# A decoder layer on one core: two gates as a block product ahead of the attention, and four output tiles begun with heads 0 to 3 behind it

## The chip, the core and the metric

The kernel runs on one core of a Trainium2 chip. Five engines work side by side, each through its own queue in order: TensorE (PE) multiplies matrices into PSUM, VectorE (DVE) and ScalarE (ACT) work element by element, GpSimd (POOL) and SyncE (SP) issue transfers here. Loading the stationary operand of a matmul is listed apart as PEld. The metric is the device time of one execution in microseconds.

## The reference

One decoder layer over 1024 tokens of width 1024, in float32. What matters here:

```python
h = rms_norm(x, norm_mix_pre)
proj = h @ w_in                    # q, k, v, u_pool, q_mem, gate logits
a = diff_attention(q, k, v, lam)   # 8 heads, two softmax maps each
a = rms_norm(a, subln_g) * (1.0 - lam_init)
y_attn = a @ w_attn_branch
y_pool = multiscale_pool(...) @ w_pool_branch
y_mem = memory_cross_attention(...) @ w_mem_branch
gates = sigmoid(gate_logits)       # 3 x 1024 columns
mix = gates[0] * y_attn + gates[1] * y_pool + gates[2] * y_mem
x = x + rms_norm(mix @ w_out, norm_mix_post)
# then the channel mixer: w_up, causal conv3, gelu gate, w_down
```

The change concerns `gates[0]`, the gate logits of the attention branch (8 tiles of 128 columns), and the product with `w_attn_branch` (8 output tiles).

## The kernel before

**Products.** Every operand of a product is split into a high and a low part (`split`, L86: a rounding copy on ScalarE, a difference on VectorE), and a product is three matmuls (`mm3`, L102): high by high, high by low, low by high. Tensors have channels on the partitions and tokens along the free axis; the 1024 tokens are two halves of 512, one PSUM bank each. A plain product of one 128-column tile of `w_in` with `h` is 2 halves x 8 depth tiles x 3 = 48 matmuls of 128x512.

**Block products.** `seven` (L198) computes a pair of such tiles in Strassen-Winograd form: depth and columns are cut in two, seven products (`product`, L175, 4 depth tiles x 3 = 12 matmuls each) take the place of eight. That is 84 matmuls for a pair in place of 96. Its weight sums (`weight_sums`, L184) are four VectorE additions; the sums of `h` were made once before (`hops`). `channels` (L1014) loads the weights of a pair and calls `seven`.

**Ahead of the attention** come, in this order: the values (block products), `channels` for the keys of heads 0 and 1, for the queries of heads 0 to 7 in four pairs (results split by `split_heads` and stored to `q_d`), and for gates 0 and 1. `marks["ahead"]` makes the weight sums of the call that follows the keys wait, on VectorE's queue, for the end of the keys' own. The weights of gate 2 are then split (`ready`, L1046).

**The attention** (L1349 on) goes over 8 heads, and in each over 4 blocks of two query tiles of 128. For a tile: `products` (L1164) gives the two score maps; `scores` (L1185) takes score plus bias and its minimum on VectorE (L1203) and the exponential on ScalarE (L1212); `combine` (L1224) joins the two maps on VectorE (L1232); one block later `turn_weights` (L1237) transposes them on TensorE and splits them, and `weigh_values` (L1255) multiplies with the values. A score map fills two banks and there are two such pairs of banks, so the products of a tile wait until the minimum of the tile before has read its map. These steps are the list `stages`; between them `weave` (L259) puts a list of `fillers`, work without a part in that chain: the keys of the next head (`head_keys`, L1105, heads 1 to 6 make those of heads 2 to 7: 48 matmuls in four steps), loads of the next values, and gates. `GATES` (L1347) says which gate fills which head: gates 2 and 3 in head 0, gate 4 in head 7. `gate` (L1135) is a generator of 8 steps of 6 matmuls, each step behind the latest scores; the first steps of gate 2 run ahead of the first scores. A scheduler orders the instructions by program order and readiness; `tc.issue_after` adds an order on one engine's queue.

**Behind the attention** gates 5, 6 and 7 are computed (L1460). Then the eight heads are loaded, scaled by their norms and split (L1470 to L1475, into `ath` and `atl`). Norms of heads 4 to 7 need the last head's squares, a trip through DRAM (`ss_d`, `head_norms`, `r_d`) and a load. `merge_heads(dt, g)` (L1446) multiplies output tile `dt` with heads 0 to 3 (g = 0) or 4 to 7 (g = 1), 24 matmuls each; tiles 0 and 1 get their first half before heads 4 to 7 are loaded. `merge(dt)` (L1493) applies the sigmoid gate and adds the other branches (`mixp_d`). Then follow the loads of `w_out` (`load_wo`, L1486) and the output projection.

## Time and profile before

| what | value |
|---|---|
| median of 3 runs | 1725.25 us (1724.72 to 1725.97) |
| the profiled execution | 1723.22 us |
| its span, first to last instruction | 1721.4 us |
| granted TensorE clock, mean | 1.000 |
| first scores of head 0 | at 601.88 us |
| first merge matmul | at 903.75 us |
| first matmul of the output projection | at 990.84 us |

How to read the profile: a line of the order in time has the start in us, the duration, the engine, the line of the kernel, the operation, what it writes and reads, the size, and in brackets how long the engine had idled before it and what ended that. A line of the groups has the count, the busy time in us and the mean in ns, and the idle time before the group. A line of the stretches has begin and end, length, and the busy time of each engine with its number of instructions, then the granted clock, the share of the transfer engines and GB/s. Durations of matmuls overlap, so the distance between starts is what a matmul takes.

### The profile page before, as it was taken

To read this page: it belongs to the slowest core of one execution; us is meant where nothing else is said; L and a number is where in the kernel's file an instruction comes from. 1 tells how busy PE (TensorE), PEld (TensorE's weight loads), DVE (VectorE), ACT (ScalarE), POOL (GpSimd) and SP (SyncE) were. 2 spreads that over 40 slices of the span, in tenths; PEclk is the share of its full clock that TensorE was granted. 3 is DMA by queue.
4 is the path that set the end of the run, shared out by engine and by line. 5 is a ranking of instruction groups with operands and counts; after the bars stand their busy time and mean duration, and the time that the engine had idled before them with its cause. 6 is when DMAs were issued, how large, how long until landed. Compare 5 with 4: busy or idle time off the path is not lost.

```text
span 1721.4 us, 22406 instructions
## 1 busy us (share of the span) xinstructions
PE 1710.9 (99%) x8106; PEld 1421.0 (83%) x8106; DVE 1241.8 (72%) x2059; ACT 890.0 (52%) x1585; POOL 45.0 (3%) x103
## 2 busy tenths in 40 slices
PE   9999999999999999999999999999999999999998
PEld 6888888888888888888888888888888888888886
DVE  7676876666665578988866555848888888878466
ACT  5434544444544467777744344645555555543453
POOL 0000000000000011111110000000000000000000
PEclk9999999999999999999999999999999999999999
DMA  8675544444874676666466670563433332583344
GB/s 276 242 253 219 163 149 156 160 141 155 257 231 153 209 228 179 179 183 170 117 215 214 204 212 38 180 217 95 126 121 93 122 101 83 199 301 102 107 150 137
DMA packets 232867, 294.41 MB, mean 171 GB/s; under 512 B 15929, under 2 KB 161590, under 8 KB 230070
## 3 DMA queue, kind: packets, MB, share of 16 engines
q1 hardware_dynamic: 229222, 285.61, 52.0%
q0 software_dynamic: 3520, 7.38, 1.2%
q8 instruction: 64, 1.05, 0.2%
q14 instruction: 45, 0.37, 0.1%
q10 hardware_dynamic: 16, 0.00, 0.0%
HBM read 201.10 MB, written 85.56 MB: 167 GB/s over the span
## 4 chain that ended last, share of the span: by engine, by line
PE 97%; DVE 2%; DMA 1%; issue 1%; ACT 0%; DVEq 0%
PE pa L103 8%; PE pa L105 8%; PE pa L104 8%; PE pb L104 5%; PE pb L103 5%; PE pb L105 5%; PE pss L1178 4%; PE poa L1267 3%; PE pd L103 2%; PE pd L104 2%; PE pd L105 2%; PE pta L1248 2%; PE pe L103 2%; PE pe L105 2%; PE pe L104 2%; PE pout L103 2%
## 5 line engine op out<-in xcount | busy, mean ns | idle before, releaser
L89 ACT ACTIVATE wpage<-s 128x512 fp32r<-128x512 f32 x136 | 85.3, 627 | 103.2 <-PE pb L105 33.6
L1655 DVE SCALAR_TENSOR_TENSOR cvt<-gv,cols,cvt 128x1023 f32<-128x1023 f32 x88 | 112.5, 1278 | 14.8 <-ACT cvt L1651 14.8
L90 DVE TENSOR_TENSOR wpage<-s,wpage 128x512 fp32r<-128x512 f32 x136 | 92.8, 688 | 39.7 <-ACT wpage L89 39.7
L1203 DVE CUSTOM_DVE_ANT_0 z<-pss,hbias 128x256 f32<-128x256 f32 (+7 forms) x128 | 94.6, 752 | 22.4 <-PE pss L1178 19.9
L1212 ACT ACTIVATE z<-z,mx 128x256 f32<-128x256 f32 (+7 forms) x128 | 98.8, 773 | 22.4 <-DVE mx L1203 22.0
L103 PE MATMUL pa<-T,wpage 128*128 128x512 f32 x264 | 102.9, 390 | 0.3 <-DVE gv L252 0.3
L105 PE MATMUL pa<-T,wpage 128*128 128x512 f32 x264 | 102.7, 389 | 0.0
L104 PE MATMUL pa<-T,wpage 128*128 128x512 f32 x264 | 102.7, 389 | 0.0
L89 ACT ACTIVATE page<-blk 128x1024 fp32r<-128x1024 f32 (+1 forms) x42 | 41.4, 989 | 86.3 <-PE pe L104 50.6
L1178 PE MATMUL pss<-ks,q 128*128 128x512 f32 (+5 forms) x384 | 83.9, 347 | 1.1 <-DVE mx L1203 1.0
L90 DVE TENSOR_TENSOR page<-blk,page 128x1024 fp32r<-128x1024 f32 (+1 forms) x42 | 47.5, 1131 | 39.5 <-ACT page L89 39.5
L1178 PEld LDWEIGHTS pss<-ks,q 128*128 128x128 f32 x384 | 63.5, 188 | 9.0 <-DVE mx L1203 3.2
L103 PE MATMUL pd<-page 128*128 128x512 f32 x176 | 68.7, 390 | 0.0
L104 PE MATMUL pd<-page 128*128 128x512 f32 x176 | 68.5, 389 | 0.0
L105 PE MATMUL pd<-page 128*128 128x512 f32 x176 | 68.3, 389 | 0.0
L103 PE MATMUL pa<-hT,wpage 128*128 128x512 f32 x168 | 65.5, 390 | 0.0
L105 PE MATMUL pa<-hT,wpage 128*128 128x512 f32 x168 | 65.4, 389 | 0.0
L104 PE MATMUL pa<-hT,wpage 128*128 128x512 f32 x168 | 65.4, 389 | 0.0
L1267 PEld LDWEIGHTS poa<-aT,v 128*128 128x128 f32 x480 | 61.2, 190 | 3.7 <-ACT srow L1294 1.8
L1267 PE MATMUL poa<-aT,v 128*128 128x256 f32 (+1 forms) x480 | 63.3, 281 | 0.0
L103 PEld LDWEIGHTS pa<-T,wpage 128*128 128x128 f32 x264 | 49.6, 188 | 11.2 <-DVE gv L252 0.7
L104 PEld LDWEIGHTS pa<-T,wpage 128*128 128x128 f32 x264 | 49.6, 188 | 10.2
(429 smaller groups left out, 4970.5 us busy)
## 6 DMA issues: line engine op xcount, KB each, us to landing
q<-q_d SPq DMA_DIRECT2D x64, 256.0 KB, 4.6
wd<-in_w_down_dram SPq DMA_DIRECT2D x22, 512.0 KB, 5.7
tw_d<-wd SPq DMA_DIRECT2D x11, 1024.0 KB, 4.0
rawv<-in_w_up_dram SPq DMA_DIRECT2D x22, 512.0 KB, 5.7
rawu<-in_w_up_dram SPq DMA_DIRECT2D x22, 512.0 KB, 4.0
ff_d<-cvt SPq DMA_DIRECT2D x22, 512.0 KB, 4.7
blk<-ff_d SPq DMA_DIRECT2D x20, 512.0 KB, 6.2
br<-tw_d SPq DMA_DIRECT2D x20, 512.0 KB, 4.2
```

Of the source, the lines that this page charges most:

```text
L89: copy = nc.scalar.activation(out=hi, in_=src, func=AF.Copy)
L90: nc.vector.tensor_tensor(out=lo, in0=src, in1=hi.bitcast(F32), op=ALU.subtract)
L103: nc.tensor.matmul(o, ah, bh, start=first, stop=False, skip_group_check=onto)
L104: nc.tensor.matmul(o, ah, bl, start=False, stop=False, skip_group_check=onto)
L105: return nc.tensor.matmul(o, al, bh, start=False, stop=last, skip_group_check=onto)
L1178: last["scores"] = nc.tensor.matmul(pss[:, i * H:i * H + m], q[:, j, c, ts], keys, start=(j == 0), stop=(j == 1))
L1203: last["min"] = nc.vector.tensor_tensor_reduce(out=halves(z[:, 0:n]), in0=pss.rearrange("p (a m) -> p a m", a=2)[:, 0:parts, 0:m], in1=hal ...
L1212: last["exp"] = nc.scalar.activation(out=z[:, 0:n], in_=z[:, 0:n], func=AF.Exp, scale=-1.0, bias=mx[:, c:c + 1], accum_out=sm if c else su ...
L1248: nc.tensor.transpose(pt[:, j * P:(j + 1) * P], zs[u][:, k * P:(k + 1) * P], ident)
L1267: nc.tensor.matmul(po[:, qs], (vh, vl)[i][:, k, :], w[j][:, ws], start=(n == 0), stop=(n == len(terms) - 1))
L1655: nc.vector.scalar_tensor_tensor(out=cv[:, sh:], in0=u[:, 0:S - sh], scalar=w, in1=cv[:, sh:], op0=ALU.mult, op1=ALU.add)
```

## The change

Gates 2 and 3 are computed by `channels` as one pair, between the keys of heads 0 and 1 and the queries, and stored to `gate_d`. The plain gates that fill the attention move up: gate 4 fills head 0, alone, and gate 5 head 7; gates 6 and 7 remain behind the attention. In head 0 one gate step and one load of values change places. The key weights of head 2 are loaded early (`fetch_keys`). In head 7 one step of gate 5 goes ahead of the last score products. Behind the attention, weights of the output tiles are loaded and split by halves (`merge_weights`); four tiles, in place of two, are multiplied with heads 0 to 3 before heads 4 to 7 are loaded, head by head; then tiles 0 and 1 take heads 4 and 5 and after that 6 and 7. Tiles 2, 3, 6 and 7 accumulate in the double banks. The last loads of `w_out` are queued behind the last load of `mixp_d`.

```diff
         marks["ahead"] = marks["c22"]
+        g = channels(C_G + 2 * P)
+        nc.sync.dma_start(out=gate_d[2:4].rearrange("e p s -> p e s"), in_=g)
         for h in range(0, NH, 2):
             split_heads(channels(h * P), q_d[h:h + 2], -0.125)
...
-        ready = {2: wsplit(chunk(w_in, C_G + 2 * P), [P, KT, P])}
-        with tc.issue_after(ready[2][2].ins):
+        ready = {4: wsplit(chunk(w_in, C_G + 4 * P), [P, KT, P])}
+        with tc.issue_after(ready[4][2].ins):
             late[0]()
...
+    fetched = {}
+
+    def fetch_keys(h):
+        w2 = [wst.tile([P, KT, P], F32R, tag=t, name=t) for t in ("wh", "wl")]
+        with tc.issue_after(last["keys"].ins):
+            for e, w in enumerate(w2):
+                nc.sync.dma_start(out=w.bitcast(F32), in_=wk_d[h, :, e])
+        return w2
...
-        wh, wl = [wst.tile([P, KT, P], F32R, tag=t, name=t) for t in ("wh", "wl")]
-        with tc.issue_after(last["keys"].ins):
-            for e, w in enumerate((wh, wl)):
-                nc.sync.dma_start(out=w.bitcast(F32), in_=wk_d[h, :, e])
+        wh, wl = fetched.pop(h) if h in fetched else fetch_keys(h)
...
-            for ins in calm if dt == 5 else ():
+            for ins in calm if dt == 6 else ():
...
-    first = gate(2)
+    first = gate(4)
...
-        ready[3] = wsplit(chunk(w_in, C_G + 3 * P), [P, KT, P])
     load_keys(1)
     last["keys"] = last["load"]
-    GATES = ((2, 3), (), (), (), (), (), (), (4,))
+    fetched[2] = fetch_keys(2)
+    gates = {}
+    GATES = ((4,), (), (), (), (), (), (), (5,))
...
-                stages.append(lambda h=h, b=b: scores(h, b, 0, ready[3][2] if (h, b) == (0, 2) else None))
+                stages.append(lambda h=h, b=b: scores(h, b, 0, None))
...
-                        products(h, b, 1)
+                        if h == NH - 1:
+                            next(gates[5])
+                            with tc.issue_after(last["gate"].ins):
+                                products(h, b, 1)
+                        else:
+                            products(h, b, 1)
...
-                        ready[4] = wsplit(chunk(w_in, C_G + 4 * P), [P, KT, P])
+                        ready[5] = wsplit(chunk(w_in, C_G + 5 * P), [P, KT, P])
...
-            for step in steps(first if dt == 2 else gate(dt), 5 if dt == 2 else 8):
+            gates[dt] = first if dt == 4 else gate(dt)
+            for step in steps(gates[dt], 5 if dt == 4 else 8):
                 fillers.insert(min(n, len(fillers)), step)
                 n += 2
+        if h == 0:
+            fillers[3:5] = fillers[4], fillers[3]
...
-    def merge_heads(dt, g):
+    def merge_weights(dt, g, own=None):
+        raw = wst.tile([P, HG, P], F32, tag="raw", name="rawm", bufs=2)
+        nc.sync.dma_start(out=raw, in_=w_attn_branch[g * HG * P:(g + 1) * HG * P, dt * P:(dt + 1) * P]
+                          .rearrange("(k p) c -> p k c", p=P))
+        if own:
+            w = own.tile([P, 2, HG, P], F32R, tag="page", name="mpage", bufs=2)
+        else:
+            w = wst.tile([P, 2, HG, P], F32R, tag=("wh", "wl")[pages[0] % 2], name="mpage")
+            pages[0] += 1
+        split(w[:, 0], w[:, 1], raw)
         if g == 0:
-            pys[dt] = wsplit(chunk(w_attn_branch, dt * P), [P, KT, P])[:2] + (bank(name="pya"), pbank(name="pya"))
-        wh, wl, *py = pys[dt]
+            if dt % 4 < 2:
+                pys[dt] = bank(name="pya"), pbank(name="pya")
+            else:
+                py = bank2(name="pya")
+                pys[dt] = py[:, 0:H], py[:, H:2 * H]
+        return w
+
+    def merge_heads(dt, w, ks):
         for i in range(2):
             hs = slice(i * H, (i + 1) * H)
-            for k in range(g * HG, (g + 1) * HG):
-                mm3(py[i], wh[:, k, :], wl[:, k, :], ath[k][:, hs], atl[k][:, hs], k == 0, k == KT - 1)
+            for k in ks:
+                mm3(pys[dt][i], w[:, 0, k % HG, :], w[:, 1, k % HG, :], ath[k][:, hs], atl[k][:, hs],
+                    k == 0, k == NH - 1)
...
-        for dt in range(5, KT):
+        for dt in range(6, KT):
             for step in steps(gate(dt), 8):
                 step()
+        ws = [merge_weights(dt, 0, sub) for dt in range(2)]
         for h in range(NH):
+            if h == 2:
+                ws += [merge_weights(dt, 0) for dt in range(2, 4)]
             if h == HG:
...
-                for dt in range(2):
-                    merge_heads(dt, 0)
+                for k in range(HG):
+                    for dt in range(4):
+                        merge_heads(dt, ws[dt], (k,))
...
-            nc.sync.dma_start(out=mp, in_=mixp_d[dt][:, hs])
+            last["gm"] = nc.sync.dma_start(out=mp, in_=mixp_d[dt][:, hs])
...
-    for dt in range(KT):
-        if dt >= 2:
-            merge_heads(dt, 0)
-        merge_heads(dt, 1)
+    ws = [merge_weights(dt, 1) for dt in range(2)]
+    for ks in ((4, 5), (6, 7)):
+        for dt in range(2):
+            merge_heads(dt, ws[dt], ks)
+            if ks[0] == 6:
+                merge(dt)
+    for dt in range(2, KT):
+        for g in range(0 if dt >= 4 else 1, 2):
+            merge_heads(dt, merge_weights(dt, g), range(g * HG, (g + 1) * HG))
         merge(dt)
...
-        for k in range(4, KT):
-            load_wo(wo, k)
+        with tc.issue_after(last["gm"].ins):
+            for k in range(4, KT):
+                load_wo(wo, k)
```

More of the change, by code (lines that the diff above doesn't have):

```diff
@@ L1493, in merge @@
     def merge(dt):
-        for i, py in enumerate(pys.pop(dt)[2:]):
+        for i, py in enumerate(pys.pop(dt)):
             hs = slice(i * H, (i + 1) * H)
```

## The prediction

> **What bounds the kernel now.** I read the page first: its busy line, its clock row and its chain.
>
> ```profile
> span 1721.4 us, 22406 instructions
> ...
> PE 1710.9 (99%) x8106; PEld 1421.0 (83%) x8106; DVE 1241.8 (72%) x2059; ACT 890.0 (52%) x1585; POOL 45.0 (3%) x103
> ...
> PEclk9999999999999999999999999999999999999999
> ...
> PE 97%; DVE 2%; DMA 1%; issue 1%; ACT 0%; DVEq 0%
> ```
>
> TensorE carries 97% of the chain, at full clock. Busy time overstates it, since pipelined matmuls overlap: one 128x512 matmul shows 0.39 us. So next I read the order in time on TensorE through the six block-product pairs ahead of the attention, from the first product to the first plain gate matmul.
>
> ```profile
> 484.93 0.39 PE L103 MATMUL pa<-hTh,wpage 128*128 128x512 f32 x1
> ...
> 580.12 0.39 PE L103 MATMUL pa<-hTh,wpage 128*128 128x512 f32 x1
> ...
> 599.16 0.39 PE L103 MATMUL pg<-hTh,wh 128*128 128x512 f32 x1
> 599.39 0.39 PE L104 MATMUL pg<-hTl,wh 128*128 128x512 f32 x1
> ```
>
> Six pairs of 84 matmuls take 599.16 - 484.93 = 114.23 us: **0.2267 us a matmul, 19.04 us a pair**, and the last pair alone takes 19.04 too. Plain gate matmuls follow at the same distance. No pair waits for weights, splits or sums, so a matmul taken out of a dense stretch is worth 0.2267 us.
>
> Is the attention dense as well? The stretches of the eight heads, cut at each head's first score matmul (the last at the end of its last gate matmul), columns PE, PEld, DVE, ACT, POOL:
>
> ```profile
> 601.88:637.44 35.56, 35.56 (x195) 30.27 (x193) 25.09 (x65) 23.16 (x55) 4.46 (x8) 1.00 0.83 241
> 637.44:669.69 32.25, 32.25 (x201) 28.08 (x200) 27.03 (x71) 24.37 (x59) 4.25 (x8) 1.00 0.64 176
> 669.69:702.02 32.33, 32.33 (x201) 28.45 (x200) 28.81 (x73) 25.74 (x63) 4.28 (x8) 1.00 0.62 175
> ...
> 766.70:799.26 32.56, 32.48 (x201) 28.09 (x200) 29.85 (x88) 25.29 (x62) 4.28 (x9) 1.00 0.68 191
> 799.26:831.52 32.26, 32.26 (x201) 28.18 (x200) 29.10 (x73) 25.18 (x62) 4.28 (x9) 1.00 0.61 161
> 831.52:863.46 31.94, 30.86 (x186) 26.69 (x185) 26.44 (x69) 23.16 (x58) 4.53 (x9) 1.00 0.30 83
> ```
>
> TensorE is covered throughout, but VectorE is busy 84 to 92% of each head, and every head is held together by filler: 48 plain matmuls (keys of the next head, or a gate) of 10.88 us, in head 0 the 84 that are left of gates 2 and 3 (12 of gate 2's 48 run before the first scores). Where filler runs out, TensorE waits for VectorE. That happens once, in head 7:
>
> ```profile
> 853.87 1.78 PE L1178 MATMUL pss<-ks,q 128*128 128x448 f32 x8
> 856.69 1.18 PE L1178 MATMUL pss<-ks,q 128*128 128x512 f32 x4 [1.03 <-DVE mx L1203]
> 857.71 0.38 PE L1248 MATMUL pta<-ident,z 128*128 128x128 f32 x2
> 857.85 1.18 PE L1178 MATMUL pss<-ks,q 128*128 128x512 f32 x4
> ```
>
> The last token block's products need the banks that the minimum (L1203) of the block before still reads.
>
> **The change part by part.**
>
> *Gates 2 and 3.* Removed: 2 x 48 = 96 plain matmuls. Added: one pair of 84. At 0.2267 us: -21.76 + 19.04 = **-2.72 us**. The pair also brings seven splits, four weight sums, six evictions, two 512 KB weight loads and one 1 MB store on the SP queue; the four neighbouring pairs hold all of that (theirs with four wide splits and two stores more) inside 19.04 us without a wait, so it costs nothing; if the cover failed, it would show as a gap between pairs. What goes on the other side are two weight splits (1.06 us ACT and 1.22 us VectorE each by the wh and wl rows below), four evictions and four stores issued by POOL.
>
> *Head 0 with 36 filler matmuls instead of 84.* Dense, it would shrink by 48 x 0.2267 = 10.88 us to 24.68 us. Its VectorE work is 25.09 us, of which one weight split goes:
>
> ```profile
> L1203 DVE CUSTOM_DVE_ANT_0 z<-pss,hbias 128x128 f32<-128x128 f32 (+7 forms) x16 | 11.6, 751 | 7.8 <-PE pss L1178 7.8
> ...
> L90 DVE TENSOR_TENSOR wl<-raw,wh 128x1024 fp32r<-128x1024 f32 x1 | 1.2, 1222 | 0.0
> L1229 DVE RECIPROCAL mx<-sm 128x1 f32<-128x1 f32 x8 | 1.2, 158 | 3.0 <-ACT z L1212 3.0
> ```
>
> 25.09 - 1.22 = 23.87 us in 24.68 would be 97% busy, more than any head shows. The 7.8 us that VectorE idles for scores are filler time and go with it; the 3.0 us for exponentials are latency and stay unless other work steps in. Bounds for the length: at 92%, the highest share above (29.85 of 32.56), 26.0 us, a loss of 1.4; at 84%, the lowest (27.03 of 32.25), 28.5 us, a loss of 3.8; at no loss 24.7. I take **+1.4 us**: head 0 starts with empty queues and ends, unlike heads 1 to 6, without the previous head's last transposes. A delay of VectorE at its end may run into head 1, as it does from each head into the next already. The row of head 7 speaks for a loss of this size: 1.03 us at one place where no filler stood.
>
> The Trainium skill, "TensorE: Matmul & The Clock Gate", Part 2, says that only weight loads are pulled ahead and matmuls stay in program order. The trace agrees: behind the wait of 1.03 us stood gate matmuls whose weights had long been split, and none stepped forward. By that rule this change takes away what hides the waits, and the sum has the loss; if matmuls could pass a waiting one, the loss would be 0 and the sum that of rival A.
>
> *Head 7.* One gate step (6 matmuls, 1.36 us) is put ahead of the last products, where the wait of 1.03 us is. The total of filler is unchanged; the six are missing a few us later, where gate 6 can follow at once, as gate 5 does now. **-1.0 us** (from -1.0 to 0).
>
> *Key weights of head 2* (two loads of 512 KB) are issued behind the keys of head 1, near 607 us, instead of at 631; gate 3's weight load (512 KB, 600.41 us) goes.
>
> ```profile
> 600.41 0.48 SPq L337 DMA_DIRECT2D raw<-in_w_in_dram  x1
> 602.09 4.71 SPq L1102 DMA_DIRECT2D ks<-k_d  x4
> 606.90 1.01 SPq L1080 DMA_DIRECT2D v<-v_d  x2
> ...
> 630.93 0.59 SPq L1111 DMA_DIRECT2D wh<-wk_d  x1
> 631.56 0.43 SPq L1111 DMA_DIRECT2D wl<-wk_d  x1
> ```
>
> Behind them wait values(1) and the queries of head 1. 512 KB more at the 241 GB/s of head 0's row is 2.2 us on loads that are needed about 20 us later: cost 0, from 0 to 2.2 if head 1 starts early on late queries.
>
> *Behind the attention.* Before: 144 gate and 48 merge matmuls stand ahead of heads 4 to 7; after: 96 and 96. The cover of the latency chain (squares, norms, r_d, rows of heads 4 to 7) stays 192 matmuls. Now:
>
> ```profile
> 889.15 1.23 DVE L90 TENSOR_TENSOR atl<-a,ath 128x1024 fp32r<-128x1024 f32 x1 [0.57 <-ACT ath L89]
> ...
> 915.45 1.23 DVE L90 TENSOR_TENSOR atl<-a,ath 128x1024 fp32r<-128x1024 f32 x1 [1.13 <-ACT ath L89]
> ```
>
> ```profile
> 903.75 0.39 PE L103 MATMUL pya<-ath,wh 128*128 128x512 f32 x1
> ...
> 914.63 0.39 PE L103 MATMUL pya<-ath,wh 128*128 128x512 f32 x1
> ...
> 916.67 0.39 PE L103 MATMUL pya<-ath,wh 128*128 128x512 f32 x1
> ...
> 990.84 0.39 PE L103 MATMUL pout<-woh,mixh 128*128 128x512 f32 x1
> ```
>
> Head 7 is split at 916.68 and first used at 916.67 + 0.23: just in time. With the new order (heads 4 and 5 for two tiles, then 6 and 7) it is wanted 24 matmuls, 5.44 us, after head 4 plus one head, so the chain gains some 4 us of slack. The early end is tighter: the merge starts one gate (10.88 us) and the 1.0 us of head 7 sooner, at 891.9 on the old axis, and the first head is ready at 890.4. The weights of tiles 2 and 3 are loaded between heads 1 and 2 and split on the queues that split the heads. I take 0; bounds 0 and +2 us, the time by which head 0 would have to slip. The 384 merge matmuls stay dense now (990.84 - 903.75 = 87.09 us = 384 x 0.2268). Sixteen half weight splits for eight whole ones add 1.6 us ACT (16 x 0.63 - 8 x 1.06) and 1.3 us VectorE (16 x 0.69 - 8 x 1.22), spread over 87 us of matmuls with VectorE at about two thirds: hidden. The output projection's last weights now wait for the last mixp load, off the path.
>
> ```profile
> L89 ACT ACTIVATE wpage<-s 128x512 fp32r<-128x512 f32 x136 | 85.3, 627 | 103.2 <-PE pb L105 33.6
> L90 DVE TENSOR_TENSOR wpage<-s,wpage 128x512 fp32r<-128x512 f32 x136 | 92.8, 688 | 39.7 <-ACT wpage L89 39.7
> ...
> L90 DVE TENSOR_TENSOR wl<-raw,wh 128x1024 fp32r<-128x1024 f32 x6 | 7.3, 1220 | 0.8 <-ACT wh L89 0.8
> L89 ACT ACTIVATE wh<-raw 128x1024 fp32r<-128x1024 f32 x6 | 6.3, 1055 | 5.1 <-PE pg L104 4.7 <-PE pya L104 0.4
> ```
>
> **Sum**: -2.72 + 1.4 - 1.0 + 0 = **-2.3 us**. The profiled execution took 1723.22 us, 1.8 more than its span; the median of the three runs is 1725.25, 2.0 higher. All terms are differences, so I set them against the median: **1722.9 us**, -0.14%. 0.2%, about what a measurement of this kernel can tell from no change, is 3.45 us.
>
> **The rivals.**
>
> *A. All dense.* The new order of head 0's filler covers every wait: -2.72 - 1.0 = -3.7 us, 1721.5, just beyond 0.2%. For it: before, head 0 loses under half a us in all its gaps; ACT and VectorE drop a split. Against it: 97% of VectorE. It decides from a loss under 0.3 us in head 0.
>
> *B. Head 0 is paced by VectorE, slower than before.* Heads 1 to 6 take 32.3 us with like work on VectorE. If each block's chain (scores, minimum, exponential, combine, transpose, split) sets the pace and head 0 needs 32.3 us as well, it loses 7.6 us: -2.72 - 1.0 + 7.6 = +3.9, **1729.1**. It is slower beyond 0.2% from a head 0 of 31.9 us on. Against it: heads 1 to 6 have 10.88 us of filler where head 0 keeps 8.16, 3 to 6 us more VectorE work, and are dense, so 32.3 is their TensorE time, not a latency.
>
> *C. Late first merge.* The four tiles begin 11.9 us sooner; if the loads of heads 0 and 1 slip behind the two extra weight loads, or tiles 2 and 3 wait for splits queued behind the heads, TensorE loses 2 us there: 1724.9, no measurable change.
>
> **How the numbers follow.** Forecast (head 0 loses 0.3 to 3.8) 0.52, A 0.28, C 0.08, B or another loss of its size 0.12. Forecast and C lie within 0.2%: faster 0.28, same 0.60, slower 0.12. The range leaves out B alone: from A less the 1.25 us between the lowest and the highest run shown (1724.72 and 1725.97), 1720.2, to the forecast with the upper bounds of head 0 and of the first merge, -2.72 + 3.8 - 1.0 + 2 = +2.1, 1727.3. The forecast's own range, with head 0 alone between its bounds, is 1721.8 to 1725.3.
>
> **What would show it.** Twelve matmuls fewer (8094, less what a trace misses). From the first pair's product to the first plain gate matmul 114.2 + 19.04 = 133.3 us: longer means the pair isn't free. Head 0, between first score matmuls, 26.0 us: 24.7 is A, 32 is B. The wait of 1.03 us at head 7's last products gone. From the first merge matmul to the first of the output projection 87.1 us: longer is C. Wrong would be the whole argument if the time moved by more than 0.2% with these four as forecast, or if a wait showed up outside these stretches.

## The result and the profile after

The changed kernel took **1728.03 us** (median of 12 runs, 1725.45 to 1732.11); the kernel before, on the same chip, 1725.14 us (12 runs, 1723.58 to 1725.97). The ratio is 1.0019, with a 95% interval from 1.0010 to 1.0028: slower by 0.19%, where 0.14% faster was forecast, and 0.7 us above the range.

The profiled execution took 1729.82 us, 1.8 more than its span. The head of its page and its chain:

```profile
span 1728.0 us, 22426 instructions
...
PE 1713.0 (99%) x8094; PEld 1420.0 (82%) x8094; DVE 1249.7 (72%) x2079; ACT 893.5 (52%) x1598; POOL 42.9 (2%) x99
...
PE 90%; DMA 4%; DVE 3%; ACT 1%; SPq 1%; issue 1%; DVEq 0%; ACTq 0%
```

The twelve matmuls are gone (8094). But the chain that ended last runs through TensorE for 90% of the span, where before it was 97%; of the rest DMA has 4%, VectorE 3%, and ScalarE and SP's queue 1% each. The stretches of the changed kernel, cut at the same events as in the prediction, show where; the columns are length, busy time of PE, PEld, DVE, ACT and POOL, granted clock, DMA share and GB/s. In order: first pair product to first gate matmul, head 0, head 1, head 7 to the first merge product, first merge product to the first of the output projection, and from there to the first transpose (pt) behind the first output row.

```profile
486.75:620.03 133.28, 133.28 (x589) 110.39 (x588) 74.57 (x106) 54.80 (x88) 2.81 (x3) 1.00 0.54 175
622.75:650.39 27.64, 27.13 (x152) 21.92 (x151) 23.84 (x64) 21.26 (x52) 3.05 (x6) 1.00 0.95 271
650.39:681.99 31.60, 31.45 (x196) 27.29 (x197) 27.24 (x71) 24.77 (x60) 4.58 (x9) 1.00 0.65 181
843.87:903.76 59.89, 59.82 (x341) 51.06 (x340) 41.82 (x102) 34.70 (x82) 8.84 (x17) 1.00 0.39 116
903.76:991.25 87.49, 87.36 (x386) 71.95 (x385) 56.76 (x73) 37.41 (x54) 0.54 (x1) 1.00 0.66 217
991.25:1018.54 27.29, 23.96 (x97) 18.55 (x96) 13.78 (x21) 10.56 (x15) 0.00 (x0) 0.94 1.09 317
```

The last stretch in the kernel before:

```profile
990.84:1012.61 21.77, 21.77 (x97) 17.97 (x96) 13.41 (x21) 9.49 (x14) 0.00 (x0) 1.00 1.07 292
```

The front does nearly what was said: up to the first merge product the changed kernel is ahead by 1.8 us (903.76 - 486.75 = 417.01 against 903.75 - 484.93 = 418.82), where the sum of the prediction, whose terms other than 0 all lie in this stretch, gave 2.3. Then one place takes 5.5 us: **96 matmuls of the first output row need 27.29 us in place of 21.77**. The other differences are small: 0.4 us in the merges, 0.7 us in all that follows, and 1.8 us ahead of the first pair product, where the two kernels are the same and 20 profiles lie between 484.8 and 486.8 us whatever the kernel. The sum is 1.8 - 1.8 + 0.4 + 5.5 + 0.7 = 6.6 us, the difference of the spans. The medians differ by 2.9, since the profiled execution of before lies 1.9 us under its median and the changed one's 1.8 over.

TensorE's order in time at that place, in the changed kernel:

```profile
996.46 0.39 PE L105 MATMUL pout<-woh,mixl 128*128 128x512 f32 x1
998.95 0.50 PE L103 MATMUL pout<-woh,mixh 128*128 128x512 f32 x1 [2.10 <-ACT woh L89]
1000.21 0.50 PE L104 MATMUL pout<-wol,mixh 128*128 128x512 f32 x1 [0.76 <-DVE wol L90]
1000.55 0.54 PE L105 MATMUL pout<-woh,mixl 128*128 128x512 f32 x1
1000.89 0.63 PE L103 MATMUL pout<-woh,mixh 128*128 128x512 f32 x1
1001.32 0.63 PE L104 MATMUL pout<-wol,mixh 128*128 128x512 f32 x1
...
1003.27 0.80 PE L104 MATMUL pout<-wol,mixh 128*128 128x512 f32 x1 [0.47 <-DVE wol L90]
```

24 products (four rows of w_out) run densely from 991.25 on; then TensorE waits for the high words of row 4, its low words, and the low words of row 5 (six products belong to a row, so 1003.27 is the 32nd). Between the waits, products stand 0.43 us apart, not 0.2267. The granted clock in stretches of 4 us (the column behind POOL):

```profile
996.00:1000.00 4.00, 1.35 (x5) 0.56 (x3) 2.00 (x3) 1.88 (x2) 0.00 (x0) 1.00 0.98 352
1000.00:1004.00 4.00, 3.32 (x8) 2.16 (x9) 3.37 (x5) 2.22 (x4) 0.00 (x0) 0.58 1.03 386
1004.00:1008.00 4.00, 4.00 (x19) 3.23 (x18) 1.57 (x2) 1.06 (x1) 0.00 (x0) 0.99 1.18 296
```

So part of the 5.5 us is a lower clock behind the waits: 0.58 for 4 us.

Why are the rows late? ScalarE's order in the changed kernel:

```profile
987.37 1.13 ACT L89 ACTIVATE mixh<-gm 128x512 fp32r<-128x512 f32 x2
993.06 0.63 ACT L1540 ACTIVATE gm<-gm 128x512 f32<-128x512 f32 x1 [4.55 <-issue]
994.38 0.63 ACT L1540 ACTIVATE gm<-gm 128x512 f32<-128x512 f32 x1 [0.69 <-DMA gm<-gate_d]
997.84 1.06 ACT L89 ACTIVATE woh<-rawo 128x1024 fp32r<-128x1024 f32 x1 [2.83 <-DMA rawo<-in_w_out_dram]
```

And the SP queue, the changed kernel first, the kernel before second:

```profile
982.26 0.33 SPq L1527 DMA_DIRECT2D rawo<-in_w_out_dram  x1
989.35 0.32 SPq L1538 DMA_DIRECT2D gm<-gate_d  x1
989.73 0.42 SPq L1539 DMA_DIRECT2D gm<-mixp_d  x1
990.24 0.38 SPq L1538 DMA_DIRECT2D gm<-gate_d  x1
990.67 1.11 SPq L1539 DMA_DIRECT2D gm<-mixp_d  x1
991.83 1.37 SPq L1527 DMA_DIRECT2D rawo<-in_w_out_dram  x3
```

```profile
982.75 0.33 SPq L1499 DMA_DIRECT2D gm<-gate_d  x1
...
985.47 0.32 SPq L1499 DMA_DIRECT2D gm<-gate_d  x1
985.83 0.43 SPq L1500 DMA_DIRECT2D gm<-mixp_d  x1
986.32 0.42 SPq L1488 DMA_DIRECT2D rawo<-in_w_out_dram  x1
```

The new order holds rows 4 to 7 until the last mixp load is out, 990.67. That alone would not be late: the loads of the last tile themselves go out 1.9 and 1.0 us ahead of the first output product (991.25), before it was 8.1 and 5.4 us. Two things can make them late. A load needs one of two gm buffers, which VectorE gives back at the end of a merge (SP's queue waits 6.7 us for that ahead of 989.35). And tiles 6 and 7 sit in one two-bank tile each, whose halves VectorE multiplies together. VectorE's multiplications of tile 6, L1541, changed, and L1502, before:

```profile
984.21 1.28 DVE L1541 TENSOR_TENSOR gm<-pya,gm 128x512 f32<-128x512 f32 x2
```

```profile
978.55 0.68 DVE L1502 TENSOR_TENSOR gm<-pya,gm 128x512 f32<-128x512 f32 x1
982.64 0.68 DVE L1502 TENSOR_TENSOR gm<-pya,gm 128x512 f32<-128x512 f32 x1
```

Before, the first half of tile 6 is multiplied 4.1 us ahead of the second; after, both come at 984.21.

### The profile page after: what moved, and what is told of

Its sections match the earlier page's. It is cut to its first block, busy times and chain, and to the rows that moved or that the text cites. A ratio compares the mean times of both kernels' runs of the same rounds, so it can differ in the third digit from the quotient of the medians.

```text
span 1728.0 us, 22426 instructions
## 1 busy us (share of the span) xinstructions
PE 1713.0 (99%) x8094; PEld 1420.0 (82%) x8094; DVE 1249.7 (72%) x2079; ACT 893.5 (52%) x1598; POOL 42.9 (2%) x99
## 4 chain that ended last, share of the span: by engine, by line
PE 90%; DMA 4%; DVE 3%; ACT 1%; SPq 1%; issue 1%; DVEq 0%; ACTq 0%
PE pa L103 8%; PE pa L105 8%; PE pa L104 8%; PE pb L103 5%; PE pb L105 5%; PE pb L104 5%; PE pss L1187 4%; PE poa L1276 3%; PE pd L103 2%; PE pd L104 2%; PE pd L105 2%; PE pta L1257 2%; PE pe L104 2%; PE pe L103 2%; PE pe L105 2%; PE pout L104 2%
## 5 line engine op out<-in xcount | busy, mean ns | idle before, releaser
L103 PE MATMUL pa<-hT,wpage 128*128 128x512 f32 x180 | 70.1, 389 | 0.0
L104 PE MATMUL pa<-hT,wpage 128*128 128x512 f32 x180 | 70.0, 389 | 0.0
L105 PE MATMUL pa<-hT,wpage 128*128 128x512 f32 x180 | 70.0, 389 | 0.0
```

The lines of the kernel that those rows point to most:

```text
L103: nc.tensor.matmul(o, ah, bh, start=first, stop=False, skip_group_check=onto)
L104: nc.tensor.matmul(o, ah, bl, start=False, stop=False, skip_group_check=onto)
L105: return nc.tensor.matmul(o, al, bh, start=False, stop=last, skip_group_check=onto)
```

## The experiments

Each run was timed beside the kernel before on the same chip; the ratio is to that. "Distance" is the time from the first pout to the first pt product, 21.77 us when nothing waits.

**The order, and the front alone.** e1 takes the order away.

```diff
-        with tc.issue_after(last["gm"].ins):
-            for k in range(4, KT):
-                load_wo(wo, k)
+        for k in range(4, KT):
+            load_wo(wo, k)
```

> The changed kernel without the order that puts the loads of w_out's rows k = 4 to 7 behind the last mixp load; all else as changed. Theory T1 (that order costs the time: in the changed profile the first pt product stands 27.3 us behind the first pout product, before it stood 21.8 behind): the loads are issued ahead of the last tile's gate and mixp loads, the distance from the first pout to the first pt product comes back to about 22 us, and the time falls by 4 to 6 us to 1722 to 1724 us. It gives part of that back (1 to 2 us) if a row whose page is still held keeps the last tile's mixp load waiting and the last merge comes late. Rival T2 (the time went elsewhere, in head 0 or in the merges; the distance is late for another reason, such as ScalarE's splits): the distance stays at 26 us or more and the time within 1 us of the changed kernel.

Measured: ratio 1.0015 (1.0007 to 1.0024), 1727.18 us; distance 26.07. The order is not the whole cause: without it most of the loss stays, as T2 has it. What holds the rows then is ScalarE's queue:

```profile
986.32 1.14 ACT L89 ACTIVATE mixh<-gm 128x512 fp32r<-128x512 f32 x2
992.52 0.63 ACT L1540 ACTIVATE gm<-gm 128x512 f32<-128x512 f32 x1 [5.07 <-issue]
995.20 0.63 ACT L1540 ACTIVATE gm<-gm 128x512 f32<-128x512 f32 x1 [2.04 <-DMA gm<-gate_d]
995.73 2.93 ACT L89 ACTIVATE woh<-rawo 128x1024 fp32r<-128x1024 f32 x3
```

All loads of w_out but one are out by 984.0 us, the last at 987.7, and a load lands at most 6.3 us after its issue; but the splits of rows 4 to 6 (woh) run at 995.73, right behind the two sigmoids of the last tile (L1540), of which the second waits for its gate load. So a late gate load makes the rows late with and without the order. e2 adds the order alone to the kernel before:

```diff
-            nc.sync.dma_start(out=mp, in_=mixp_d[dt][:, hs])
+            last["gm"] = nc.sync.dma_start(out=mp, in_=mixp_d[dt][:, hs])
...
-        for k in range(4, KT):
-            load_wo(wo, k)
+        with tc.issue_after(last["gm"].ins):
+            for k in range(4, KT):
+                load_wo(wo, k)
```

> The kernel before with one thing of the change added: the loads of w_out's rows k = 4 to 7 behind the last mixp load. T1: the distance from the first pout to the first pt product grows from 21.8 us to 25 to 28 us and the kernel is 3 to 6 us slower than the kernel before (1728 to 1731 us). T2: the distance stays near 22 us and the time within 1 us of 1725.

Measured: 1.0007 (0.9998 to 1.0016), distance 21.77. In the old tail the order costs the output projection nothing, so T1 falls as the only cause. e3 keeps the order for rows 6 and 7:

```diff
-        with tc.issue_after(last["gm"].ins):
-            for k in range(4, KT):
+        for k in range(4, KT):
+            with tc.issue_after(last["gm"].ins) if k >= 6 else nullcontext():
                 load_wo(wo, k)
```

> The changed kernel with that order kept for the rows k = 6 and 7 alone; rows 4 and 5 are loaded as soon as their pages allow. T1: most of the wait goes, since the long wait of the changed profile (2.1 us) is for a row's high words that are split at 997.84 us, the first of the four; the distance is 22 to 24 us and the time 1722.5 to 1725 us, the lower end if rows 6 and 7 come in time. T2: no more than 1 us below the changed kernel.

Measured: 1.0007 (0.9999 to 1.0016), distance 24.35, a little over T1's 22 to 24. e4 has the new front and the old tail; its edit starts from the changed kernel, and the tail's main lines are:

```diff
-        ws = [merge_weights(dt, 0, sub) for dt in range(2)]
...
-                for k in range(HG):
-                    for dt in range(4):
-                        merge_heads(dt, ws[dt], (k,))
+                for dt in range(2):
+                    merge_heads(dt, 0)
```

> Only the part of the change up to the end of the attention: the pair of gates 2 and 3 ahead, gate 4 in head 0 with the early key weights of head 2, gate 5 in head 7 with one step in the last wait; behind the attention the tail of the kernel before (gates 6 and 7, two tiles begun with heads 0 to 3, w_out's rows in the old order). By the spans of the two profiles the pair gives -2.72, the heads 0 and 1 lose 2.3, head 7 gives -1.0: -1.4 us, if the shorter work behind the attention (two output tiles and no third gate while the norms of the last heads come) covers VectorE's and ScalarE's tail. T1 expects 1722.5 to 1725 us with that cover, and 4 us or more above it without: a wait then appears in front of the first merge product. T2 (the loss is in the front): 1726 us or more with no wait there.

Measured: 1.0013 (1.0004 to 1.0022), distance 21.77. The front gives its 1.7 us here as well (first pair product to first merge product 417.17), and the merges then lose 3.4: 90.49 us from the first merge product to the first output product, where 87.09 is dense. TensorE's waits there:

```profile
903.46 0.50 PE L104 MATMUL pya<-atl,wh 128*128 128x512 f32 x1 [0.18 <-DVE atl L90]
905.75 0.50 PE L103 MATMUL pya<-ath,wh 128*128 128x512 f32 x1 [0.38 <-ACT ath L89]
...
928.20 0.50 PE L105 MATMUL pya<-ath,wl 128*128 128x512 f32 x1 [1.14 <-DVE wl L90]
```

With a gate less behind the attention, two tiles don't cover heads and weights: more tiles have to be begun there (three were not tried).

**The two-bank tile.** e5 takes the two-bank tiles from tiles 6 and 7 (2 and 3 keep theirs):

```diff
-            if dt % 4 < 2:
+            if dt < 2 or dt >= 4:
                 pys[dt] = bank(name="pya"), pbank(name="pya")
```

> The changed kernel with output tiles 6 and 7 in two single banks each (as tiles 0, 1, 4 and 5 are, and as all eight are in the kernel before) in place of one two-bank tile; the order on w_out's loads stays. Theory T3 (from the first four runs: the order alone costs nothing without the changed tail, and without the order the changed tail still loses 4.3 us; so the two-bank tile is the cause: VectorE multiplies both halves of tile 6 only after the second half's products, the gm buffers come free late, the last tile's gate and mixp loads and its sigmoids come late, and on ScalarE's queue the splits of w_out's rows 4 to 7 stand behind those sigmoids): the multiplications of tile 6 come apart by about half a tile, the distance from the first pout to the first pt product falls from 27.3 to 24 us or less, and the time by 3 to 4 us below the changed kernel. Rival T1 (the order on the loads is the cause in the changed tail): the distance stays at 26 us or more, the time within 1 us of the changed kernel.

Measured: 1.0009 (1.0000 to 1.0018), distance 23.48; the multiplications of tile 6 come apart by 1.3 us (982.94 and 984.27), not by half a tile, and the time is 1.7 us below the changed kernel by the ratios, not 3 to 4: T3 holds in part. e6 is e5 without the order:

> As the run with two banks, and the order that puts w_out's rows 4 to 7 behind the last mixp load is taken away as well. T3: the distance from the first pout to the first pt product comes to 21.8 to 22.5 us, and the time to 1.0 to 2.0 us below the kernel before (the front's -1.8 from pair, heads and last wait, by the spans, with no loss behind it). T1: it is the same as taking away the order alone, 26 us.

Measured: 0.9998 (0.9989 to 1.0007), 1723.15 us, distance 21.77. The loss in the output projection is gone; the 1.0 to 2.0 us below the kernel before are not seen in the times. e7 puts two-bank tiles into the kernel before:

```diff
-            pys[dt] = wsplit(chunk(w_attn_branch, dt * P), [P, KT, P])[:2] + (bank(name="pya"), pbank(name="pya"))
+            py = bank2(name="pya") if dt >= 6 else None
+            py = (bank(name="pya"), pbank(name="pya")) if dt < 6 else (py[:, 0:H], py[:, H:2 * H])
+            pys[dt] = wsplit(chunk(w_attn_branch, dt * P), [P, KT, P])[:2] + py
```

> The kernel before with tiles 6 and 7 in a two-bank tile each, nothing else. T3: the distance from the first pout to the first pt product grows from 21.8 to 24 us or more, the time by 2 to 4 us. Rival T4 (the two-bank tile matters only together with the smaller weight pages or the order of the changed tail): distance and time stay as before within 1 us.

Measured: 1.0000 (0.9992 to 1.0009), distance 21.76: T4. e8 is the old front with the new tail, which then has gates 5 to 7 in it; the line in which its tail differs from the changed kernel's:

```diff
-        for dt in range(6, KT):
+        for dt in range(5, KT):
             for step in steps(gate(dt), 8):
                 step()
```

> The front of the kernel before (gates 2 and 3 in head 0, gate 4 in head 7, gates 5 to 7 behind the attention) with the tail of the change: four tiles begun with heads 0 to 3, half pages of weights, two-bank tiles 2, 3, 6 and 7, the order on w_out's loads. T3: the same loss in the output projection as in the changed kernel, a distance of 26 to 28 us, and 4 to 6 us slower than the kernel before, since the front has no part in it. Rival T2 (the front shifts the weights' loads and so makes the loss): a distance near 22 us and the time of before within 1 us.

Measured: 1.0025 (1.0016 to 1.0033), distance 26.11. The tail makes the loss without the new front, 4.3 of the 5.5 us. In the changed kernel, then, the loss is 5.5 us with order and two-bank tile, 4.3 with the tile, 1.7 with the order, 0 with neither; in the old tail each alone costs 0.

**The front's own terms.** e9 and e10 are e6 with one or no gate step ahead of head 0; the products go among its blocks. The diff is e9's; e10 leaves the loop out, weaves 7 steps, and the first scores follow the pair at once.

```diff
-    for _ in range(2):
+    for _ in range(1):
         next(first)
...
-            for step in steps(gates[dt], 5 if dt == 4 else 8):
+            for step in steps(gates[dt], 6 if dt == 4 else 8):
```

> The run with two banks and the free order (1719.7 us span in its profile), and in front of head 0 one step of gate 4 in place of two; the other step (6 matmuls, 1.36 us) goes among head 0's blocks. Theory H1 (head 0 is paced by the chain of VectorE and ScalarE that starts with its first scores, and PE has too little beside it; the head's products stand 27.64 us where 24.68 us are PE's): the first scores come 1.36 us earlier, the chain too, and of the 2.1 us of small losses in head 0 about 1.0 to 1.4 us are filled: first gate matmul to head 1's first scores 30.36 before, 29.0 to 29.4 now; the time 0.5 to 1.4 us below the two-bank free run. Rival H2 (the losses are single hand-overs that stay with another order of the queue): no change within 0.3 us in that distance.

> The same with no step of gate 4 in front of head 0: both (2.72 us) go among its blocks. H1: the first scores come 2.7 us earlier but head 0's bias is ready only 1.85 us after the last pair product, so the chain starts 1.9 us earlier; the distance from the first product behind the pair to head 1's first scores falls by 1.5 to 2.1 us, if nothing else waits. H2: no change within 0.3 us, or worse by the wait for the bias.

Measured: 1.0002 (0.9993 to 1.0010) and 1.0010 (1.0001 to 1.0019). From the end of the pair to head 1's first scores, e6 needs 30.36 us, e9 29.97 and e10 30.85, where H1 gave 29.0 to 29.4 for e9 and still less for e10; up to head 2's first scores e6 needs 61.98 us (618.57 to 680.55), e9 62.09, e10 63.23. H1 falls: what e9 gains in head 0 is lost again in head 1. In head 0 of e9 TensorE waits twice for VectorE's minimum, 0.98 and 0.38 us, which it does not in e6; the longer one:

```profile
625.31 1.21 PE L1187 MATMUL pss<-ks,q 128*128 128x512 f32 x4 [0.98 <-DVE mx L1212]
```

e11 is e6 without the step in head 7's wait:

```diff
-                            next(gates[5])
-                            with tc.issue_after(last["gate"].ins):
-                                products(h, b, 1)
+                            products(h, b, 1)
```

> The run with two banks and the free order, without the one step of gate 5 that the change puts into the wait of head 7's last products; that step goes where the weaving puts it. The prediction's term of -1.0 us: the wait of 1.0 us for VectorE's maximum comes back at the place where the kernel before has it, the distance from head 7's first scores to the first merge product grows from 59.89 to 60.8 to 61.0 us, the time by 0.9 to 1.1 us. Rival: the step only moves the wait to another place, no change within 0.3 us.

Measured: 1.0010 (1.0001 to 1.0019). The wait is back, and head 7's first scores to the first merge product need 61.35 us (842.02 to 903.37) in place of 59.89, a little more than the 60.8 to 61.0 expected:

```profile
867.18 1.20 PE L1187 MATMUL pss<-ks,q 128*128 128x512 f32 x4 [1.03 <-DVE mx L1212]
```

e12 is e6 once more:

> The same kernel as the run with two banks and the free order, timed once more, since its spans say -2.1 us against the kernel before and its times -0.4 us with an interval from -1.9 to +1.2. If the spans are right: a ratio of 0.998 to 0.9995, and both sets together below 1. If the front's gain is not in the time: a ratio of 0.9997 to 1.0005.

Measured: 1.0003 (0.9994 to 1.0012), distance 21.76; the span from the first pair product on is 1234.9 us (1721.2 - 486.35), before 1236.5. In two profiles the version is 1.6 and 2.1 us ahead, in the times of 22 runs it is not; the two profiled executions are the fastest and the second fastest of their sets.

**Half pages, or both steps together.** e13 (on e6) and e14 (on the changed kernel) merge tiles 4 to 7 with whole weights; `merge_whole` loads, splits and multiplies all eight heads of a tile as the kernel before does, into the banks that the tile has in e6 or in the changed kernel:

```diff
-    for dt in range(2, KT):
-        for g in range(0 if dt >= 4 else 1, 2):
-            merge_heads(dt, merge_weights(dt, g), range(g * HG, (g + 1) * HG))
+    for dt in range(2, KT):
+        if dt < 4:
+            merge_heads(dt, merge_weights(dt, 1), range(HG, NH))
+        else:
+            merge_whole(dt)
         merge(dt)
```

> The run with two banks and the free order, and tiles 4 to 7 merged with whole weights (8 heads of a tile in one load and one split, as the kernel before has them) in place of two half pages each. Theory M (half pages make w_out's rows late: the two raw buffers turn over twice as often, the first row is loaded at about 969 us and not at 961): the first row is loaded by 965 us, the distance from the first pout to the first pt product is 21.8 us, no wait in the first output row; and if a thin margin in that place ate the front's 1.8 us in part of the executions, the time is 0.5 to 1.8 us below the kernel before. Rival N (the half pages do nothing; the front's gain is not lost there): first row near 969 us, time as the two-bank free run, 0.0 to 0.3 us from the kernel before; a wait of 1 us or more in front of tile 4's products would also undo it, since its whole pages must come free at once.

> The changed kernel, its order on w_out's loads and its two-bank tiles kept, with whole weights for tiles 4 to 7. M: the distance from the first pout to the first pt product falls from 27.3 us to 22 to 24 us, since rows 0 to 3 are in early and only rows 4 to 7 are late; 3 to 5 us below the changed kernel. N: 26 us or more, the time of the changed kernel within 1 us.

Measured: e13 1.0002 (0.9993 to 1.0011), distance 22.29; e14 1.0029 (1.0018 to 1.0041), distance 30.27. e14 has 6 runs, the others 11. The first row of w_out does go out at 963 us now, but M falls: rows 0 to 3 were never late, and in e14 the last tile's second gate load comes even 0.5 us behind the first output product. e15 puts the edits of e2 and e7 together:

> The kernel before with both the order on w_out's loads and two-bank tiles 6 and 7; whole weights as it has them. M: the two together use up more of the margin than each alone, but without the half pages the distance stays at 21.8 to 23 us and the time within 1.2 us of the kernel before. N (order and tile together are enough): 26 us or more, and 4 us or more slower.

Measured: 1.0009 (1.0000 to 1.0018), distance 23.34: 1.6 us, between M and N. So the two steps together use up the old tail's margin, but not as far as the new tail's.

**The buffers.** e16 is the changed kernel, order and two-bank tiles kept, with three more gm buffers from space that is free until the output projection:

```diff
+    gmstack = ExitStack()
+    gmp = gmstack.enter_context(tc.tile_pool(name="gmp", reuse_waits="tile", bufs=3, side="right"))
...
-            gm2 = gq.tile([P, 2, H], F32, tag="t", name="gm2")
+            gm2 = (gq if (2 * dt + i) % 5 < 2 else gmp).tile([P, 2, H], F32, tag="t", name="gm2")
...
         load_wo(woa, k)
+    gmstack.close()
     dstack.close()
```

> The changed kernel, its order and its two-bank tiles kept, with five buffers for the gate and mixp loads of the merges in place of two. Theory L (the merges lag by the two buffers, and the order makes w_out's rows 4 to 7 wait for that): the last tile's loads go out more than 12 us ahead of the first output product (1.9 us before), so the order holds nothing back; the distance from the first pout to the first pt product falls from 27.3 us to 21.8 to 23 us, and the time by 4 to 5 us below the changed kernel. Rival (ScalarE's queue, or PE's pages, or the DMA engines make the rows late whatever the buffers): 25 us or more, the time within 1 us of the changed kernel.

> The run with two banks and the free order, with five buffers as well. L: the distance is 21.8 us with several us of margin, so the executions that lost 0.4 to 1.0 us here lose nothing; the time is 0.5 to 1.8 us below the kernel before. If the front's gain is not in the times at all: within 0.4 us of the kernel before.

Measured: e16 **0.9988 (0.9979 to 0.9997), 1721.71 us**, distance 21.76; e17 (the same on e6) 0.9992 (0.9983 to 1.0001), 1722.51 us, distance 21.76. The SP queue of e16, and its output projection in the columns of above:

```profile
968.28 0.32 SPq L1540 DMA_DIRECT2D gm<-gate_d  x1
968.64 0.43 SPq L1541 DMA_DIRECT2D gm<-mixp_d  x1
971.95 12.55 SPq L1529 DMA_DIRECT2D rawo<-in_w_out_dram  x7
```

```profile
901.96:989.00 87.04, 87.04 (x386) 72.07 (x384) 55.21 (x72) 37.55 (x56) 0.54 (x1) 1.00 0.75 252
989.00:1010.76 21.76, 21.76 (x97) 17.97 (x96) 13.96 (x22) 10.19 (x15) 0.00 (x0) 1.00 1.09 302
```

The last tile's loads go out 20.7 us ahead of the first output product, so the order holds nothing back, and TensorE is dense through merges and output projection. The spans from the first pair product on say the same as the times: 1234.0 us in e16 (1718.8 - 484.81) and 1234.4 in e17 (1719.5 - 485.15) against 1236.5 in the kernel before. e18 gives the five buffers to the kernel before:

> The kernel before with five buffers for the merges' gate and mixp loads, nothing else. Theory L: its output projection loses nothing with two (21.8 us from the first pout to the first pt product), so five give nothing there: time within 0.6 us of the kernel before, and the 2.3 us of the changed kernel with five buffers are the front's. Rival: the buffers themselves give 1 us or more in the kernel before too.

Measured: 1.0001 (0.9992 to 1.0010), distance 21.76. The buffers alone give nothing where nothing is late.

The tails side by side. Row 4's low words are used by the 26th product, 5.67 us (25 x 0.2267) after the first pout; the fourth column says when VectorE has them ready.

| kernel | last gate load, us ahead of the first pout | distance, us | row 4's low words ready, us after the first pout | ratio |
|---|---|---|---|---|
| before | 5.4 | 21.77 | 3.0 | 1 |
| e2 order | 5.2 | 21.77 | 4.0 | 1.0007 |
| e7 tile | 5.0 | 21.76 | 3.9 | 1.0000 |
| e15 both | 5.0 | 23.34 | 4.5, row 5 late | 1.0009 |
| changed | 1.0 | 27.29 | 8.9 | 1.0019 |
| e1 without order | 1.3 | 26.07 | 8.4 | 1.0015 |
| e14 changed, whole pages | 0.5 behind it | 30.27 | 9.8 | 1.0029 |
| e5 without tile | 2.6 | 23.48 | 6.9 | 1.0009 |
| e6 neither | 2.6 | 21.77 | 4.8 | 0.9998 |
| e16 changed, five buffers | 20.7 | 21.76 | 5.6 | 0.9988 |
| e17 neither, five buffers | 18.9 | 21.76 | 3.8 | 0.9992 |

## Why the prediction was wrong

**The pair was right.** 133.28 us from the first pair product to the first gate matmul, 133.3 forecast.

**Head 7 was right.** The wait of 1.03 us is gone, -1.0 forecast; e11 puts its worth at 1.46 us (61.35 - 59.89), 0.46 more than the term: the wait and some 0.4 us behind it.

**Head 0 was right in kind, small in size.** 26.0 us were forecast, 27.64 stand there, inside the bounds. Heads 0 and 1 together take 59.24 us in place of 67.81 (35.56 + 32.25): 8.57 saved of 10.88, a loss of 2.3 in place of 1.4. The prediction reads VectorE as 84 to 92% busy in each head; that holds for heads 1 to 6, while head 0 itself stood at 71% (25.09 of 35.56) and head 7 at 83%. After the change VectorE is 86% busy in head 0 (23.84 of 27.64), between the two shares that made the bounds. Neither A (24.7) nor B (32) happened; that the time came out near B's 1729.1 is chance, the loss lies elsewhere. e9 and e10 show that one or two gate steps more among its blocks do not help.

**The merges were right.** 87.49 us, 87.1 forecast; C did not happen.

**The step that failed** is this one: "The output projection's last weights now wait for the last mixp load, off the path." It stood in the sum at nothing, without a bound, and without a name for the work that covers it. What was wrong is "off the path", more than the order itself: 4.3 of the 5.5 us stay without the order (e1), and the two-bank tiles, the larger step, have no term in the sum at all. The margin could be read in the trace of before, where ScalarE splits rows 4 to 7 only around the first output product (990.84):

```profile
990.51 1.99 ACT L89 ACTIVATE woh<-rawo 128x1024 fp32r<-128x1024 f32 x2
992.58 2.35 DVE L90 TENSOR_TENSOR wol<-rawo,woh 128x1024 fp32r<-128x1024 f32 x2
```

Row 4's low words, the first of the two, are ready 3.0 us after that product, 2.7 us ahead of their use. The profile of the changed kernel has them 3.2 us late:

```profile
998.93 1.23 DVE L90 TENSOR_TENSOR wol<-rawo,woh 128x1024 fp32r<-128x1024 f32 x1 [2.00 <-ACT woh L89]
```

The 5.5 us of the first output row are about as large as the forecast's error (1728.03 - 1722.9 = 5.1): without them the profiled execution would have stood at 1724.3 us. The prediction's own sign of being wrong came true as well: a wait showed up outside its four stretches.

What the runs showed in its place is not that step alone, which costs nothing in the old tail (e2). Three parts of the change use up one margin. Four tiles are begun with heads 0 to 3, so tiles 0 to 3 end half a tile apart, faster than two gm buffers turn over: e6 has the last gate load 2.6 us ahead of the output projection where the kernel before has 5.4. The two-bank tiles bring both halves of tile 6 to VectorE at once, and the load goes out at 1.0 us. Rows 4 to 7 then wait for it, their splits in ScalarE's queue behind the last tile's sigmoids (e1), and with the order their loads as well. That the loss hangs on the two buffers is shown by e16: order, tiles and pages as in the changed kernel, five buffers in place of two, and the loss is gone. That it does not need the half pages of tiles 4 to 7 is shown by e14. That it is the distance of the first four tiles that makes the merges lag is argued from these rows; three tiles, or four with another spacing, were not tried, nor the new order of the heads and the half pages of tiles 0 to 3 by themselves.

With the loss away, the front's gain is in the times: e16 is 2.3 us below the kernel before (interval 0.5 to 3.6), and e18 shows that the buffers alone don't give it. e17, with the same front, is 1.5 below, and its interval (-0.2 to 2.9) holds 0. That 2.3 is also the prediction's sum is in part luck: by the traces the front gives 1.8, since heads 0 and 1 lose 0.9 us more than their term and head 7 gives 0.5 more than its own. **The changed kernel with five gm buffers is ahead of both**, by 0.1% and, by the ratios, 0.3%.

Two things stay open. The kernel without the order and without two-bank tiles 6 and 7 (e6, e12) loses nothing in its profiles, but its times are not below the kernel before; e9 and e11, with the same tail, lose 0.9 us in the output projection, where row 4 has under 1 us of margin in e6, so other executions may lose there too. That was not shown: no profile of a late execution of e6 was taken. A thin margin alone does not do it: row 4 has 0.1 us in e16 (5.6 of 5.67) and nothing is lost, but there the splits stand behind the last tile's own end (mixh) and behind no late load. And e14 is later than the changed kernel as its last gate load goes out 1.5 us later against the first output product; what makes that load later with whole pages was not followed up.

## What to carry to other kernels

A load that is put behind another in a queue costs nothing only if its first use is far enough away: find that use in the trace of before, write the margin in us beside the step, and add up everything in the same change that delays what it now waits for. Work that is begun early may end at shorter distances (here that is argued, not shown), so count again the buffers that turned over once per end. When one edit seems guilty, try it alone in the old kernel as well: here each of two costs nothing there, and the cheap cure was in a third place.

## What the runs showed of the hardware

A short wait of TensorE can cost more than its own length, where the granted clock falls behind it. In the changed kernel TensorE was busy 1.35 us of 4, and the clock of the next 4 us was 0.58, with products 0.43 us apart; by that clock up to 1.7 us more go (4 x 0.42, an estimate that takes the whole stretch for products). The profile of e14, with waits of 2.95, 0.76 and 1.52 us, has 0.78, 0.50 and 0.87 in three stretches:

```profile
998.00:1002.00 4.00, 2.75 (x7) 1.49 (x7) 2.62 (x4) 3.15 (x5) 0.00 (x0) 0.78 1.02 414
1002.00:1006.00 4.00, 2.82 (x7) 2.24 (x8) 3.49 (x3) 1.06 (x1) 0.00 (x0) 0.50 1.17 306
1006.00:1010.00 4.00, 4.00 (x17) 3.25 (x16) 0.00 (x0) 0.81 (x1) 0.00 (x0) 0.87 1.20 290
```

e1, with waits of 0.74, 1.62 and 1.10 us, kept the full clock in its profile:

```profile
996.00:1000.00 4.00, 1.64 (x7) 1.07 (x7) 3.67 (x6) 4.00 (x6) 0.00 (x0) 1.00 0.25 101
1000.00:1004.00 4.00, 2.90 (x13) 2.10 (x12) 4.00 (x5) 1.49 (x3) 0.00 (x0) 1.00 0.91 278
```

The length of the waits does not decide it: e8 waited only 1.04 and 0.77 us there, was busy 2.38 us of the 4 from 996 to 1000, more than e1's 1.64, and its clock in the next 4 us was 0.57. What does decide it, no run here shows. The changed kernel's 12 runs span 6.7 us, with mean clocks of 0.997 to 1.000, the 12 of the kernel before 2.4 us; that the clock makes this scatter is not shown.

The Trainium skill, "TensorE: Matmul & The Clock Gate", Part 1, gives 426.7 ns between matmuls of N = 512 at the low clock, and says that the clock falls after at least one idle window of about 3.4 us. The trace agrees with the first number (0.43 us). The second differs: no wait of TensorE in the first output row was longer than 2.95 us in these profiles, and the clock fell.
